# Matmul, GELU, matmul on one core: another order for the first contraction slices of the first product

## The chip, the core and the metric

The kernel runs on one core of a Trainium2 chip. The core has five engines with queues of their own: TensorE (PE, with weight loads as PEld), VectorE (DVE), ScalarE (ACT), GpSimd (POOL) and SyncE (SP). They meet through semaphores. DMA transfers are issued from SP's and POOL's queues here. The metric is the device time of one execution in microseconds (us); a kernel's figure is the median over its runs.

## The reference

```python
m, k, n, p = 1024, 1024, 2048, 1024        # a: m x k, b: k x n, c: n x p, all fp32
h = np.matmul(a, b)
h = 0.5 * h * (1 + np.tanh(np.sqrt(2 / np.pi) * (h + 0.044715 * h ** 3)))
return np.matmul(h, c).astype(np.float32)
```

## The kernel before

Everything is computed transposed: `hT`, the hidden matrix with its 2048 columns on the partitions, in 16 tiles of 128, and the 1024 rows of `a` as two halves of 512 (index `h`, 0 and 1). The contraction of the first product has 8 slices of 128 (`k`). `aT[:, h, k]` is a slice of a half, transposed; `b1[:, k]` holds the first 1024 columns of `b`, `b2` the others, `c_sb` all of `c`, in bf16.

There are three stages, in an order written out by hand: each engine runs its instructions in the order in which the program names them.

1. Hidden tiles 0 to 7 (from `b1`) for both halves, by ordinary matmuls (`mm1`, line 126): 8 tiles x 8 slices x 2 halves = 128 matmuls of 128x128 by 128x512. GELU on ACT writes `hT`.
2. Hidden tiles 8 to 15 (from `b2`) by a scheme with seven products in place of eight (class `Seven`, function `seven`; the matmuls are at line 229). Its sums and differences `t1` to `t4` (of parts of `aT`) and `s1` to `s4` (of parts of `b2`) are DVE work. `t1`, `t2` and `t3` are done in stage 1.
3. The second product, by the same scheme.

Stage 1 is what the change concerns. Its input comes in two ways. SP's queue loads fp32 data into staging tiles (`sta` for `a`, `stb` for `b`), and DVE or ACT cast it to bf16 (lines 118, 135, 136). POOL's queue loads with a cast to bf16 on the way, straight into `b1`, `b2`, `c_sb` and the pieces `a1` (lines 98, 105, 109, 112). The copy at line 85, into `gate`, makes POOL wait for SP's load of slice 1 of `b` before it issues the first of its own.

A slice of `a` is transposed on PE, four transposes of 128x128 for 512 rows, into a PSUM bank (`pt`), and DVE copies the bank into `aT` (`turn0`, line 116, for staged slices; `turn`, line 154, for two slices loaded by POOL). PSUM has eight banks, and a tile takes a whole one; a bank is used again when its reader is done.

The order before: slices 0 to 3 of half 0 for tiles 0 to 6, slice by slice as they arrive through SP, into seven banks; these sums leave PSUM for `half` (`leave`, line 145), tile 7 following. Then half 1: all eight slices, from POOL's loads, with GELU from PSUM. Then half 0's slices 4 to 7, each tile's sum added to `half` on DVE (line 258) and passed through GELU. SP loads slices 0 to 3 of half 0 of `a` and slices 0 to 3 of `b1`; POOL all else.

After stage 1, `seven` begins with four products into banks `X` (snapped to SBUF by ACT, line 268), then four into banks `Y`, to which DVE adds the snapped ones (line 273).

Of the kernel before, what the change touches and what calls it, by code (L numbers as in the profile page):

```python
# [9 lines left out]
F32 = mybir.dt.float32  # L10
F32R = mybir.dt.float32r
BF16 = mybir.dt.bfloat16
AF = mybir.ActivationFunctionType
ADD = mybir.AluOpType.add
# [5 lines left out]
def kernel(ctx, tc, a, b, c, out):  # L20
    nc = tc.nc
# [3 lines left out]
    H = 512  # L25
    KT = K // 128
    NT = N // 128

    av = a.rearrange("(mt p) k -> p mt k", p=128)
    bv = b.rearrange("(kt p) n -> p kt n", p=128)  # L30
# [9 lines left out]
    def slot(tag, shape, dt, name):  # L40
        return big.tile(shape, dt, name=name, tag=tag)

    def bank(i, shape=(128, H), dt=F32, name="ps"):
        return pp.tile(list(shape), dt, name=name, tag=f"bank{i}", padded_shape=None)

    def pieces(tag, bufs, shape, dt, name):
        return small.tile(shape, dt, name=name, tag=tag, bufs=bufs)
# [3 lines left out]
    ident = consts.tile([128, 128], BF16, name="ident")  # L51
    make_identity(nc, ident)
    gate = consts.tile([128, 1], F32, name="gate")
# [4 lines left out]
    aT = slot("a", [128, 2, KT, H], BF16, "aT")  # L58
    b1 = slot("b1", [128, KT, 1024], BF16, "b1")
    b2 = slot("b2", [128, KT, 1024], BF16, "b2")  # L60


    N0 = 7
    stb = slot("x0", [128, 4, 1024], F32, "stb")
    sta = slot("x1", [128, 4096], F32, "sta")

    def slice_a(k, n):
        return sta[:, ds(k * H, n * H)].rearrange("p (mt c) -> p mt c", mt=4)

    def load_a(k, n):  # L70
        nc.sync.dma_start(out=slice_a(k, n), in_=av[:, 0:4, ds(k * 128, n * 128)])  # L71

    def load_b(k, c0=0, w=1024):
        nc.sync.dma_start(out=stb[:, k, ds(c0, w)], in_=bv[:, k, ds(c0, w)])  # L74

    load_a(0, 1)
    load_b(0, 0, H)
    load_b(0, H, H)
    load_a(1, 1)
    load_b(1)  # L80
    load_a(2, 2)
    load_b(2)
    load_b(3)

    nc.gpsimd.tensor_copy(gate, stb[:, 1, 0:1])  # L85
    nc.scalar.activation(g, warm[:, 0:1], AF.Gelu_apprx_tanh)
    wps = bank(7, name="warmps")
    for _ in range(8):
        nc.tensor.matmul(wps, warm[:, 0:128], warm, start=True, stop=True)


    KH = KT // 2

    def load_half(h, k0):
        sts = []
        for j in range(0, 4, 2):
            st = pieces("m", 4, [128, 2, H], BF16, "a1")
            nc.gpsimd.dma_start(out=st, in_=av[:, 4 * h + j:4 * h + j + 2, ds(k0 * 128, H)])  # L98
            sts.append(st)
        return sts  # L100

    a10 = load_half(1, 0)
    a11 = load_half(1, KH)
    for k in range(KH, KT):
        nc.gpsimd.dma_start(out=b1[:, k], in_=bv[:, k, 0:1024])
    a01 = load_half(0, KH)
    for n in range(2):
        for k in range(0, KT, 4):
            nc.gpsimd.dma_start(out=b2[:, k:k + 4, ts(n, H)],
                                in_=bv[:, k:k + 4, ds(1024 + n * H, H)])  # L110
    for t in range(0, NT, 2):
        nc.gpsimd.dma_start(out=c_sb[:, t:t + 2], in_=cv[:, t:t + 2])  # L112

    ps = [bank(t) for t in range(N0)]

    def turn0(k, n):
        ab = pieces("ab", 2, [128, 4, n * 128], BF16, "ab")
        nc.vector.tensor_copy(ab, slice_a(k, n))
        pt = bank(7, (128, n, H), BF16, "pt")
        for i in range(n):  # L120
            for j in range(4):
                nc.tensor.transpose(pt[:, i, ts(j, 128)], ab[:, j, ts(i, 128)], ident)
        for i in range(n):
            nc.vector.tensor_copy(aT[:, 0, k + i], pt[:, i])

    def mm1(p, t, h, ks, k0=0, k1=KT):
        for k in ks:
            nc.tensor.matmul(p, b1[:, k, ts(t, 128)], aT[:, h, k],  # L128
                             start=(k == k0), stop=(k == k1 - 1))

    turn0(0, 1)
    for k in range(KH):
        for c0 in (0, 256) if k == 0 else (0,):
            w = 256 if k == 0 else H
            nc.scalar.activation(b1[:, k, ds(c0, w)], stb[:, k, ds(c0, w)], AF.Copy)  # L135
        nc.vector.tensor_copy(b1[:, k, H:], stb[:, k, H:])
        for t in range(N0):
            mm1(ps[t], t, 0, (k,), 0, KH)
        if k < 2:
            turn0(k + 1, k + 1)  # L140


    half = slot("x3", [128, 8, H], F32, "half")

    def leave(t, p):
        if t in (1, 3, 5):
            nc.vector.tensor_copy(half[:, t], p)
        else:
            nc.scalar.activation(half[:, t], p, AF.Copy)

    for t in range(N0):
        leave(t, ps[t])

    def turn(sts, h, k, i):
        pt = bank(i, (128, 2, H), BF16, "pt")
        for n in range(2):
            for j in range(4):
                nc.tensor.transpose(pt[:, n, ts(j, 128)],  # L158
                                    sts[j // 2][:, j % 2, ts((k + n) % KH, 128)], ident)
        nc.vector.tensor_copy(aT[:, h, k:k + 2], pt)  # L160

    def gelu(t, h, p):
        nc.scalar.activation(hT[h][:, t], p, AF.Gelu_apprx_tanh)  # L163

    turn(a10, 1, 0, 0)
    p7 = bank(7)
    mm1(p7, 7, 0, range(KH), 0, KH)
    leave(7, p7)
    turn(a10, 1, 2, 1)
    B1 = (2, 3, 4, 5, 6, 7, 0, 1)  # L170
    ps = []
    for t in range(3):
        ps.append(bank(B1[t]))
        mm1(ps[t], t, 1, range(2))
    for t in range(3):
        mm1(ps[t], t, 1, range(2, KH))


    class Seven:
# [47 lines left out]
        def product(self, p, l, r, j, start, c0=0, w=H):  # L227
            for k in range(self.kt):
# [4 lines left out]
    x = [slot(f"x{i}", [128, 2, 4, H], F32R, "x1") for i in range(3)]  # L233
    one = Seven(4, [[b2[:, 0:4, 0:H], b2[:, 4:8, 0:H]], [b2[:, 0:4, H:], b2[:, 4:8, H:]]],
                [[aT[:, 0, 0:4], aT[:, 1, 0:4]], [aT[:, 0, 4:8], aT[:, 1, 4:8]]],
                [x[i][:, 0] for i in range(3)] + [None], [x[i][:, 1] for i in range(3)] + [None])
    one.t1()

    for t in range(3, 8):
        if t == 5:  # L240
            turn(a11, 1, KH, 0)
            turn(a11, 1, KH + 2, 1)
        ps.append(bank(B1[t]))
        mm1(ps[t], t, 1, range(KH))
    one.t3()
    one.t2()


    for t in range(8):
        mm1(ps[t], t, 1, range(KH, KT))  # L250
        gelu(t, 1, ps[t])
        if t in (3, 5):
            turn(a01, 0, KH + t - 3, B1[t - 3])
    C1 = (3, 5, 2, 4, 6, 7, 0, 1)
    for t in range(8):
        p = bank(C1[t])
        mm1(p, t, 0, range(KH, KT), KH)
        nc.vector.tensor_tensor(out=half[:, t], in0=p, in1=half[:, t], op=ADD)  # L258
        gelu(t, 0, half[:, t])
    x.append(slot("x3", [128, 2, 4, H], F32R, "x1"))  # L260
    one.s[3], one.t[3] = x[3][:, 0], x[3][:, 1]

    X = (2, 3, 4, 5)
    Y = (6, 7, 0, 1)

    def snap(tag, p, name):
        st = pieces(tag, 4, [128, H], F32, name)
# [8 lines left out]
    def seven(w, done, between):  # L276

        (A11, A12), (A21, A22) = w.A
        (B11, B12), (B21, B22) = w.B
        px = [bank(i) for i in X]  # L280
        p1, v, u = {}, {}, {}
# [4 lines left out]
        for j in range(4):  # L286
            p = bank(Y[j])
            w.product(p, A12, B21, j, True)
            done(0, 0, j, plus(p, p1[j]))
        between("P2")  # L290
        py = [bank(i) for i in Y]
        for j in range(4):
# [119 lines left out]
```

## Time and profile before

| | us |
|---|---|
| median of 6 runs | 122.08 (121.64 to 123.05) |
| the profiled execution | 121.93 |
| its span | 120.2 |
| PE busy | 111.3 (93%) |
| DVE busy | 89.1 (74%) |
| ACT busy | 50.8 (42%) |
| POOL busy | 16.3 (14%) |

The span is the time between the first and the last instruction that the profile shows; the execution's own time is 1.7 us longer. Busy shares are means over stages with different limits: PE is seldom idle after the first part, so that DVE's 74% says nothing on its own. What a change in stage 1 is worth is read from the waits in stage 1 and from what follows it without a gap. By the page, PE's clock is granted in full in all 40 slices of the span. 16.34 MB moved by DMA, of which POOL's queue took 8.91 MB and SP's 7.34 MB, the stores among the latter.

In an answer of the timeline a line has the start in us, the duration in us, the engine, the line of the kernel, the operation with output and inputs, and in brackets the engine's idle time before it with what ended that. A pipelined group of matmuls is one line, with its count.

### The profile page before, as it was taken

Reading aid. Unit: us, or ns where it says so; the run is one execution under the profiler, and the core shown is the slowest. Engines: PE = TensorE matmul, PEld = TensorE weight load, DVE = VectorE, ACT = ScalarE, POOL = GpSimd, SP = SyncE. Lnnn points to the kernel's source line nnn. Section 1 sums busy time; section 2 is a strip of 40 time slices with the busy share of each in tenths; the row PEclk is TensorE's granted clock in tenths of the full one; section 3 lists DMA queues with packets and bytes.
Section 4 is the critical chain, followed back from the end, with each engine's and each line's share of the span. In section 5 each row is a group of like instructions: output and inputs, shape, how many; then the busy total and the mean of one; then the engine's idle time right before and its main releaser. Section 6 shows DMA issues by size and latency. Waiting matters only on the chain.

```text
span 120.2 us, 1435 instructions
## 1 busy us (share of the span) xinstructions
PE 111.3 (93%) x536; PEld 71.3 (59%) x536; DVE 89.1 (74%) x97; ACT 50.8 (42%) x82; POOL 16.3 (14%) x29
## 2 busy tenths in 40 slices
PE   6775889999999999999999999999999999999970
PEld 2122445644544445888887444468888888888840
DVE  0235587497338899977779999969999996892480
ACT  4112461006547689946769536900012595100000
POOL 2008907843243000000000000000000000000000
PEclk9999999999999999999999999999999999999999
DMA  3799999999999999998000000072000002004695
GB/s 97 196 343 393 161 168 210 208 203 206 206 207 212 210 214 209 211 212 159 4 3 0 0 5 0 0 262 87 0 0 0 0 5 87 0 0 175 242 350 193
DMA packets 11110, 16.34 MB, mean 136 GB/s; under 512 B 736, under 2 KB 5856, under 8 KB 11104
## 3 DMA queue, kind: packets, MB, share of 16 engines
q0 software_dynamic: 6496, 8.91, 42.5%
q1 hardware_dynamic: 4608, 7.34, 17.2%
q8 instruction: 4, 0.07, 0.2%
q14 instruction: 2, 0.02, 0.0%
HBM read 20.97 MB, written 4.19 MB: 209 GB/s over the span
## 4 chain that ended last, share of the span: by engine, by line
PE 71%; DMA 16%; DVE 6%; SPq 1%; issue 1%; POOL 1%; ACT 1%; DVEq 0%; ACTq 0%
PE ps L229 51%; PE ps L128 18%; DMA stb<-in_b_dram 6%; DMA out_dram<-ot 5%; DMA a<-in_a_dram 5%; DVE x L187 4%; PE pt L158 2%; DVE ot L273 2%; SPq L74 1%; SPq L71 1%; POOL a L98 1%; DVE ot L358 1%; ACT u L268 1%; POOL gate L85 0%; DVEq L273 0%
## 5 line engine op out<-in xcount | busy, mean ns | idle before, releaser
L128 PE MATMUL ps<-aT,b 128*128 128x512 bf16 x128 | 29.1, 379 | 3.1 <-ACT b L135 2.1
L229 PE MATMUL ps<-x,s 128*128 128x512 f32 x128 | 29.6, 391 | 0.0
L229 PEld LDWEIGHTS ps<-x,s 128*128 128x128 f32 x128 | 24.0, 188 | 5.1
L128 PEld LDWEIGHTS <-b 128*128 128x128 bf16 x128 | 12.1, 98 | 17.0 <-ACT b L135 3.2
L229 PE MATMUL ps<-x,x 128*128 128x512 f32 x64 | 14.8, 389 | 0.0
L229 PE MATMUL ps<-c_sb,hT 128*128 128x512 bf16 x64 | 14.0, 379 | 0.0
L229 PEld LDWEIGHTS ps<-x,x 128*128 128x128 f32 x64 | 12.0, 188 | 2.5
L268 ACT ACTIVATE v<-ps 128x512 f32<-128x512 f32 x8 | 4.8, 599 | 17.1 <-PE ps L229 17.1
L163 ACT ACTIVATE hT<-ps 128x512 bf16<-128x512 f32 x12 | 6.8, 594 | 11.3 <-PE ps L128 11.3
L229 PE MATMUL ps<-x 128*128 128x512 f32 x48 | 11.3, 394 | 0.0
L229 PEld LDWEIGHTS <-hT 128*128 128x128 bf16 x64 | 6.2, 98 | 7.6 <-issue 0.3
L229 PEld LDWEIGHTS ps<-x 128*128 128x128 f32 x48 | 9.0, 188 | 2.0
L187 DVE TENSOR_TENSOR x<-c_sb 128x1024 fp32r<-128x1024 bf16 x8 | 9.2, 1216 | 0.0
L273 DVE TENSOR_TENSOR ot<-ps,v 128x512 f32<-128x512 f32 x8 | 5.3, 686 | 4.6 <-DMA out_dram<-ot 3.8
L258 DVE TENSOR_TENSOR half<-ps,half 128x512 f32<-128x512 f32 x8 | 5.5, 692 | 3.2 <-PE ps L128 2.9
L160 DVE COPY aT<-pt 128x1024 bf16<-128x1024 bf16 x6 | 4.1, 689 | 5.1 <-PE pt L158 5.1
L273 DVE TENSOR_TENSOR ot<-ps,u 128x512 f32<-128x512 f32 x8 | 5.4, 691 | 3.0 <-ACT u L268 3.0
L163 ACT ACTIVATE hT<-ot 128x512 bf16<-128x512 f32 x12 | 6.9, 623 | 1.1 <-DVE ot L273 1.1
L229 PE MATMUL ps<-aT,b 128*128 128x512 bf16 x32 | 7.1, 379 | 0.0
L112 POOL DMA_DIRECT2D c_sb<-in_c_dram x8 | 5.7, 713 | 9.8 <-DMA b<-in_b_dram 8.9
L268 ACT ACTIVATE p<-ps 128x512 f32<-128x512 f32 x8 | 4.6, 594 | 4.8 <-PE ps L229 4.8
L135 ACT ACTIVATE b<-stb 128x512 bf16<-128x512 f32 (+1 forms) x5 | 2.6, 541 | 9.2 <-DMA stb<-in_b_dram 9.2
(45 smaller groups left out, 114.6 us busy)
## 6 DMA issues: line engine op xcount, KB each, us to landing
c_sb<-in_c_dram POOLq DMA_DIRECT2D x8, 512.0 KB, 19.6
out_dram<-ot SPq DMA_DIRECT2D x16, 256.0 KB, 2.1
b<-in_b_dram POOLq DMA_DIRECT2D x4, 512.0 KB, 12.6
stb<-in_b_dram SPq DMA_DIRECT2D x3, 512.0 KB, 8.5
a<-in_a_dram POOLq DMA_DIRECT2D x6, 256.0 KB, 7.2
b<-in_b_dram POOLq DMA_DIRECT2D x4, 256.0 KB, 9.1
sta<-in_a_dram SPq DMA_DIRECT2D x2, 256.0 KB, 4.2
stb<-in_b_dram SPq DMA_DIRECT2D x2, 256.0 KB, 4.9
```

What stands on the lines that cost most here:

```text
L71: nc.sync.dma_start(out=slice_a(k, n), in_=av[:, 0:4, ds(k * 128, n * 128)])
L112: nc.gpsimd.dma_start(out=c_sb[:, t:t + 2], in_=cv[:, t:t + 2])
L128: nc.tensor.matmul(p, b1[:, k, ts(t, 128)], aT[:, h, k], start=(k == k0), stop=(k == k1 - 1))
L135: nc.scalar.activation(b1[:, k, ds(c0, w)], stb[:, k, ds(c0, w)], AF.Copy)
L158: nc.tensor.transpose(pt[:, n, ts(j, 128)], sts[j // 2][:, j % 2, ts((k + n) % KH, 128)], ident)
L160: nc.vector.tensor_copy(aT[:, h, k:k + 2], pt)
L163: nc.scalar.activation(hT[h][:, t], p, AF.Gelu_apprx_tanh)
L187: nc.vector.tensor_tensor(out=dst[:, r], in0=x[:, r], in1=y[:, r], op=op)
L229: nc.tensor.matmul(p[:, ds(c0, w)], l[:, k, ts(j, 128)], r[:, k, ds(c0, w)], start=(start and k == 0), stop=(k == self.kt - 1), skip_group ...
L258: nc.vector.tensor_tensor(out=half[:, t], in0=p, in1=half[:, t], op=ADD)
L268: nc.scalar.activation(st, p, AF.Copy)
L273: nc.vector.tensor_tensor(out=ot, in0=p, in1=st, op=ADD)
```

## The change

Stage 1 takes its work in another order, with other loads. Stage 2 and 3 differ only in the banks `X` and `Y`.

- Half 0 goes first with one slice only, slice 0, for all eight tiles (`first`); these sums go to `half`.
- Then half 1 with all eight slices, tiles 0 to 6 slice by slice (`begin`, and the loop from 2 to `KT`), tile 7 at the end.
- Then slices 1 to 7 of half 0 (`rest`), added to `half` as before.
- SP now loads slice 0 of half 0 of `a`, all slices of half 1 and all eight slices of `b1`, in fp32; DVE and ACT cast them. A second staging tile for `b` takes the place of `x2`. The last piece of `a` for half 1 reuses the place of the first two in `sta`.
- POOL loads slices 1 to 7 of half 0 of `a`, then `b2` and `c` as before. The copy into `gate` waits for slice 5 of `b`.
- `t3` stands behind the loop, `t1` and `t2` behind the last transposes of half 0.

```diff
-    stb = slot("x0", [128, 4, 1024], F32, "stb")
+    stb = [slot(f"x{i}", [128, 4, 1024], F32, "stb") for i in (0, 2)]
+    at = {(0, 0): 0, (1, 0): 1, (1, 1): 2, (1, 2): 3, (1, 4): 5, (1, 6): 0}
...
-    load_a(0, 1)
+    load_a(0, 0, 1)
     load_b(0, 0, H)
+    load_a(1, 0, 1)
     load_b(0, H, H)
-    load_a(1, 1)
+    load_a(1, 1, 1)
     load_b(1)
-    load_a(2, 2)
+    load_a(1, 2, 2)
     load_b(2)
     load_b(3)
-
-    nc.gpsimd.tensor_copy(gate, stb[:, 1, 0:1])
+    load_a(1, 4, 2)
+    load_b(4)
+    load_b(5)
+
+    nc.gpsimd.tensor_copy(gate, stb[1][:, 1, 0:1])
...
+    a0 = {}
+    for k, n in ((1, 3), (4, 4)):
         for j in range(0, 4, 2):
+            st = pieces("v", 4, [128, 2, n * 128], BF16, "a0")
+            nc.gpsimd.dma_start(out=st, in_=av[:, j:j + 2, ds(k * 128, n * 128)])
...
+    def turn(h, k, n, i, get):
+        pt = bank(i, (128, n, H), BF16, "pt")
+        for m in range(n):
+            for j in range(4):
+                nc.tensor.transpose(pt[:, m, ts(j, 128)], get(k + m, j), ident)
+        nc.vector.tensor_copy(aT[:, h, k:k + n], pt)
+
+    def cast_a(h, k, n):
         ab = pieces("ab", 2, [128, 4, n * 128], BF16, "ab")
+        nc.vector.tensor_copy(ab, slice_a(h, k, n))
+        return lambda q, j: ab[:, j, ts(q - k, 128)]
+
+    def turn_cast(h, k, n, i):
+        turn(h, k, n, i, cast_a(h, k, n))
...
+    def first(t, i):
+        p0[t] = bank(i)
+        mm1(p0[t], t, 0, (0,), 0, 1)
+
+    def begin(t, i, ks):
+        p1[t] = bank(i)
+        mm1(p1[t], t, 1, ks)
+
+    turn_cast(0, 0, 1, 7)
+    cast_b(0, 0, 256)
+    cast_b(0, 256, 256)
+    for t in range(4):
+        first(t, t)
+        leave(t, p0[t])
+    turn_cast(1, 0, 1, 6)
+    for t, i in enumerate((4, 5, 7, 6)):
+        begin(t, i, (0,))
+    cast_b(0, H, H, nc.vector)
+    a11 = cast_a(1, 1, 1)
+    for t in range(4, 8):
+        first(t, t - 4)
+    leave(4, p0[4])
+    leave(5, p0[5], nc.vector)
+    begin(4, 0, (0,))
+    cast_b(1, 0, H)
+    turn(1, 1, 1, 1, a11)
+    cast_b(1, H, H, nc.vector)
+    leave(6, p0[6])
+    leave(7, p0[7], nc.vector)
+    for t in range(5):
+        mm1(p1[t], t, 1, (1,))
+    begin(5, 1, (0, 1))
+    begin(6, 2, (0, 1))
+    turn_cast(1, 2, 2, 3)
+    load_a(1, 6, 2)
+    load_b(6)
+    load_b(7)
+    for k in range(2, KT):
+        cast_b(k, 0, H)
+        cast_b(k, H, H, nc.vector)
+        for t in range(7):
+            mm1(p1[t], t, 1, (k,))
+            if k == KT - 1:
+                gelu(t, 1, p1[t])
+        if k in (3, 5):
+            turn_cast(1, k + 1, 2, 3)
...
+    one.t3()
+    begin(7, 4, range(KT))
+    gelu(7, 1, p1[7])
...
+    turn(0, 1, 1, 3, get)
+    turn(0, 2, 2, 5, get)
+    R = (7, 6, 0, 1, 5, 4, 3, 2)
+    for t in range(4):
+        rest(t, R[t], (1,))
+    for t in range(4):
+        rest(t, R[t], (2, 3))
+    turn(0, 4, 2, 3, get)
+    turn(0, 6, 2, 2, get)
     one.t1()
-    for t in range(3, 8):
-        if t == 5:
-            turn(a11, 1, KH, 0)
-            turn(a11, 1, KH + 2, 1)
...
     one.t2()
+    rest(4, R[4], (1, 2, 3))
     for t in range(8):
+        rest(t, R[t], range(1 if t > 4 else 4, KT))
+        nc.vector.tensor_tensor(out=half[:, t], in0=p0r[t], in1=half[:, t], op=ADD)
         gelu(t, 0, half[:, t])
...
-    X = (2, 3, 4, 5)
-    Y = (6, 7, 0, 1)
+    X = (7, 6, 0, 1)
+    Y = (5, 4, 3, 2)
```

More of the change, by code (lines that the diff above doesn't have):

```diff
@@ L60, with slice_a, load_a @@
     b2 = slot("b2", [128, KT, 1024], BF16, "b2")
-    N0 = 7
-    stb = slot("x0", [128, 4, 1024], F32, "stb")
+    stb = [slot(f"x{i}", [128, 4, 1024], F32, "stb") for i in (0, 2)]
     sta = slot("x1", [128, 4096], F32, "sta")
[L67 to L71, printed above, removed]
+    at = {(0, 0): 0, (1, 0): 1, (1, 1): 2, (1, 2): 3, (1, 4): 5, (1, 6): 0}
+    def slice_a(h, k, n):
+        return sta[:, ds(at[h, k] * H, n * H)].rearrange("p (mt c) -> p mt c", mt=4)
+    def load_a(h, k, n):
+        nc.sync.dma_start(out=slice_a(h, k, n), in_=av[:, 4 * h:4 * h + 4, ds(k * 128, n * 128)])
     def load_b(k, c0=0, w=1024):
-        nc.sync.dma_start(out=stb[:, k, ds(c0, w)], in_=bv[:, k, ds(c0, w)])
-    load_a(0, 1)
+        nc.sync.dma_start(out=stb[k // 4][:, k % 4, ds(c0, w)], in_=bv[:, k, ds(c0, w)])
+    load_a(0, 0, 1)
     load_b(0, 0, H)
+    load_a(1, 0, 1)
     load_b(0, H, H)
-    load_a(1, 1)
+    load_a(1, 1, 1)
     load_b(1)
-    load_a(2, 2)
+    load_a(1, 2, 2)
     load_b(2)
     load_b(3)
-    nc.gpsimd.tensor_copy(gate, stb[:, 1, 0:1])
+    load_a(1, 4, 2)
+    load_b(4)
+    load_b(5)
+    nc.gpsimd.tensor_copy(gate, stb[1][:, 1, 0:1])
     nc.scalar.activation(g, warm[:, 0:1], AF.Gelu_apprx_tanh)
@@ L89 @@
         nc.tensor.matmul(wps, warm[:, 0:128], warm, start=True, stop=True)
-    KH = KT // 2
-    def load_half(h, k0):
-        sts = []
+    a0 = {}
+    for k, n in ((1, 3), (4, 4)):
         for j in range(0, 4, 2):
[L97 to L106, printed above, removed]
+            st = pieces("v", 4, [128, 2, n * 128], BF16, "a0")
+            nc.gpsimd.dma_start(out=st, in_=av[:, j:j + 2, ds(k * 128, n * 128)])
+            for i in range(2):
+                for m in range(n):
+                    a0[k + m, j + i] = st[:, i, ts(m, 128)]
     for n in range(2):
@@ L112, with cast_b @@
         nc.gpsimd.dma_start(out=c_sb[:, t:t + 2], in_=cv[:, t:t + 2])
-    ps = [bank(t) for t in range(N0)]
-    def turn0(k, n):
-        ab = pieces("ab", 2, [128, 4, n * 128], BF16, "ab")
[L118 to L124, printed above, removed]
+    def turn(h, k, n, i, get):
+        pt = bank(i, (128, n, H), BF16, "pt")
+        for m in range(n):
+            for j in range(4):
+                nc.tensor.transpose(pt[:, m, ts(j, 128)], get(k + m, j), ident)
+        nc.vector.tensor_copy(aT[:, h, k:k + n], pt)
+    def cast_a(h, k, n):
+        ab = pieces("ab", 2, [128, 4, n * 128], BF16, "ab")
+        nc.vector.tensor_copy(ab, slice_a(h, k, n))
+        return lambda q, j: ab[:, j, ts(q - k, 128)]
+    def turn_cast(h, k, n, i):
+        turn(h, k, n, i, cast_a(h, k, n))
+    def cast_b(k, c0, w, eng=None):
+        src, dst = stb[k // 4][:, k % 4, ds(c0, w)], b1[:, k, ds(c0, w)]
+        if eng is nc.vector:
+            nc.vector.tensor_copy(dst, src)
+        else:
+            nc.scalar.activation(dst, src, AF.Copy)
     def mm1(p, t, h, ks, k0=0, k1=KT):
@@ L129, in mm1, with leave @@
                              start=(k == k0), stop=(k == k1 - 1))
[L131 to L140, printed above, removed]
     half = slot("x3", [128, 8, H], F32, "half")
-    def leave(t, p):
-        if t in (1, 3, 5):
+    def leave(t, p, eng=None):
+        if eng is nc.vector:
             nc.vector.tensor_copy(half[:, t], p)
@@ L149, in leave @@
             nc.scalar.activation(half[:, t], p, AF.Copy)
[L151 to L160, printed above, removed]
     def gelu(t, h, p):
         nc.scalar.activation(hT[h][:, t], p, AF.Gelu_apprx_tanh)
[L165 to L176, printed above, removed]
+    p0, p1 = {}, {}
+    def first(t, i):
[42 more added lines that the diff above has]
+            turn_cast(1, k + 1, 2, 3)
     class Seven:
@@ L236, with get, rest @@
                 [x[i][:, 0] for i in range(3)] + [None], [x[i][:, 1] for i in range(3)] + [None])
-    one.t1()
-    for t in range(3, 8):
-        if t == 5:
-            turn(a11, 1, KH, 0)
-            turn(a11, 1, KH + 2, 1)
-        ps.append(bank(B1[t]))
-        mm1(ps[t], t, 1, range(KH))
-    one.t3()
+    one.t3()
+    begin(7, 4, range(KT))
+    gelu(7, 1, p1[7])
+    def get(k, j):
+        return a0[k, j]
+    def rest(t, i, ks):
+        if t not in p0r:
+            p0r[t] = bank(i)
+        mm1(p0r[t], t, 0, ks, 1)
+    p0r = {}
+    turn(0, 1, 1, 3, get)
[7 more added lines that the diff above has]
+    turn(0, 6, 2, 2, get)
+    one.t1()
     one.t2()
+    rest(4, R[4], (1, 2, 3))
     for t in range(8):
[L250 to L258, printed above, removed]
+        rest(t, R[t], range(1 if t > 4 else 4, KT))
+        nc.vector.tensor_tensor(out=half[:, t], in0=p0r[t], in1=half[:, t], op=ADD)
         gelu(t, 0, half[:, t])
```

## The prediction

> **What bounds the kernel now.** I read the chain of waits first, to see which stretch is paced by what. Columns: start us, us, what.
>
> ```profile
> 2.72 6.71 DMA stb<-in_b_dram
> ...
> 10.69 6.12 DMA a<-in_a_dram
> ...
> 23.89 6.04 PE ps L128 x28
> ...
> 32.55 8.63 PE ps L128 x40
> 41.18 60.71 PE ps L229 x272
> ```
>
> Until 16.8 us loads set the pace; then TensorE works without a gap to 101.9. The 272 products of the second stage go at 60.71 / 272 = 0.223 us each: a later first product (line 229) makes the end later by as much, unless it fills a gap, and there is none. So one number decides: when that first product starts. The PE's timeline (start us, us, engine, line, operation) says when, and what happened before:
>
> ```profile
> 4.94 0.40 PE L122 MATMUL pt<-ident,ab 128*128 128x128 bf16 x4
> 6.18 1.04 PE L128 MATMUL ps<-aT,b 128*128 128x512 bf16 x4 [0.84 <-ACT b L135]
> 7.67 0.82 PE L128 MATMUL ps<-aT,b 128*128 128x512 bf16 x3 [0.45 <-DVE b L136]
> 8.46 0.40 PE L122 MATMUL pt<-ident,ab 128*128 128x128 bf16 x4
> 10.14 1.69 PE L128 MATMUL ps<-aT,b 128*128 128x512 bf16 x7 [1.29 <-ACT b L135]
> 11.99 0.62 PE L122 MATMUL pt<-ident,ab 128*128 128x128 bf16 x8 [0.16 <-DVE ab L118]
> 13.12 3.18 PE L128 MATMUL ps<-aT,b 128*128 128x512 bf16 x14 [0.52 <-DVE aT L124]
> ...
> 41.02 7.07 PE L229 MATMUL ps<-aT,b 128*128 128x512 bf16 x32
> ```
>
> The first product starts at 41.02. Fourteen matmuls take 3.18 with the last one's own 0.38, so one costs (3.18 - 0.38) / 13 = 0.2155; a transpose costs (0.62 - 0.22) / 7 = 0.057. From 8.46 to 41.02, 121 matmuls (26.1) and 60 transposes (3.4) are done, so stalls are 32.56 - 29.5 = 3.1 us: 2.4 of it the waits in brackets and that for `a` at 16.86 (0.44), the rest drained pipelines. There is little to win.
>
> The DVE timeline gives the prices that matter:
>
> ```profile
> 7.97 0.43 DVE L118 CAST ab<-sta 128x512 bf16<-128x512 f32 x1 [0.36 <-DMA sta<-in_a_dram]
> 8.89 0.42 DVE L124 COPY aT<-pt 128x512 bf16<-128x512 bf16 x1 [0.49 <-PE pt L122]
> 11.02 0.91 DVE L118 CAST ab<-sta 128x1024 bf16<-128x1024 f32 x1 [1.14 <-DMA sta<-in_a_dram]
> ...
> 17.41 0.69 DVE L160 COPY aT<-pt 128x1024 bf16<-128x1024 bf16 x1 [0.26 <-PE pt L158]
> ```
>
> Windows of half a microsecond give the DMA rate (last two columns: DMA share, GB/s):
>
> ```profile
> 3.50:4.00 0.50, 0.50 (x3) 0.15 (x1) 0.43 (x1) 0.00 (x0) 0.00 (x0) 1.00 0.63 53
> 7.50:8.00 0.50, 0.33 (x2) 0.21 (x3) 0.14 (x2) 0.00 (x0) 0.00 (x0) 1.00 0.98 299
> 10.00:10.50 0.50, 0.36 (x2) 0.21 (x3) 0.00 (x0) 0.09 (x1) 0.50 (x1) 1.00 1.05 422
> 12.00:12.50 0.50, 0.50 (x8) 0.43 (x8) 0.00 (x0) 0.26 (x1) 0.50 (x2) 1.00 0.82 143
> ```
>
> Summing such windows and comparing with the waits for SP's loads: the bytes of `b` slice 1 are in at 8.06 and its user starts at 9.46; the next `a` piece 9.45 and 11.02; slice 2 10.72 and 12.24. So a load lands some 1.4 us after its bytes.
>
> **What the Trainium skill says.** "TensorE: Matmul & The Clock Gate", Part 2, Step-by-step: only weight loads are pulled ahead, matmuls stay in program order. So a matmul waiting for a transposed slice holds everything behind it. The trace agrees: at 12.92 weights are loaded while the matmuls wait for the copy until 13.12. "DMA: Bandwidth & Descriptors", Issuing engines are not separate DMA queues: SP's and POOL's transfers share the same engines. The trace agrees: the rate drops from 422 to 143 GB/s when SP's loads give way to POOL's (which read fp32 and are counted as bf16 written). The same page, Anatomy of one DMA: a fixed cost of about 2 us, mostly completion; here I see the 1.4 above.
>
> **The change part by part.** Matmuls and transposes are the same in number (128 and 64). What moves is the order. I walk it with the prices above, 0.03 from PE to DVE (transposes end 8.86, copy 8.89) and about 0.05 back (cast ends 8.40, transposes 8.46).
>
> Loads. SP's list grows from 3.15 to 6.55 MB: all of `b1` and the whole second half of `a`, plus one slice of the first half. Cumulated after the old rates (0.42 MB/us for `b`, about 0.32 for 512-byte pieces of `a`) plus 1.4: `a` (1,0) about 7.15, `b` 0's second half 7.9, `a` (1,1) 8.7, `b` 1 10.1, `a` (1,2) 11.4, `b` 2 12.7, `b` 3 13.9, `a` (1,4) 15.3, `b` 4 16.5, `b` 5 17.8, `a` (1,6) 19.2, `b` 6 20.4, `b` 7 21.7, up to 23.3 if POOL's traffic takes half. The (1,6) piece waits at SP, with `b` 6 and 7 behind it, for casts done by 7.6, ahead of its turn: nothing. POOL's gate moves to `b` 5: its loads start at 18.3 instead of 9.9, and four for the rest of `a` go first (0.72 each); bytes at 0.4 MB/us, they land at about 24 and 26.5. `b2` follows by about 37, `c` at the old time, since the bytes read are the same.
>
> Start. The first slice is as before: four matmuls at 6.18. Then `a` (1,0): cast 7.18 to 7.61, transposes 7.65, copy 8.09 to 8.51, four matmuls of the second half at 8.56. Before stood at 8.46 with three more matmuls done and four fewer transposes: 0.1 + 0.65 - 0.23 = 0.52 lost. ACT's four evacuations (2.06 for four) hide behind this.
>
> First stalls. `first(4..7)` ends 10.29. `begin(4)` reuses bank 0, so it waits for `leave(4)` (mm end 9.83 + 0.60): 0.19. The turn of (1,1) waits for `leave(5)` on DVE (10.05 to 10.68): 0.03; then copy 11.16 to 11.58, and five matmuls at 11.62: stall 0.66. Two `begin` of two matmuls fill 12.70 to 13.56.
>
> The three turns of two slices, (1,2), (1,4), (1,6): each stands directly ahead of matmuls that need it. Transposes issue in 0.45, the last result comes 0.2 later, copy 0.69, semaphores: the stall is 0.93 each, 2.8 together. Casts for them are covered: (1,2) is cast 12.63 to 13.54, after `leave(7)` and just in time. So matmuls run 14.96 to 17.98, 19.36 to 22.38, 23.76 to 26.78. Every load above is there before its cast would hold a matmul, by 0.8 us (`b` 1) or more and by 1.3 for a late `b` 7, so the extra casts (ACT 0.63, DVE 0.43 a slice) cost nothing; without that cover, its lateness one for one.
>
> Rest. `begin(7)` to 28.5, turn of (0,1): stall 0.21, as the second turn covers most. `rest` for four tiles to 31.98; the last turns are covered by three matmuls of tile 4. The two late loads are 4.5 and 5.5 us early. `t1` and `t2` on DVE end at 38.4 and the eight additions, at about 0.62 back to back as at line 273 (four in 2.48), end at 43.4, with the last matmul at 42.4 anyway; DVE's `s1`, `s2` and first sum follow to 48.6, and the product that needs that bank comes at 49.3. So no stall there, by 0.7 (before: 0.6).
>
> Sum of stalls after 8.56: 0.19 + 0.03 + 0.66 + 0.02 + 2.8 + 0.21 = 3.9, against 3.1. First product: 8.56 + 124 x 0.2155 + 56 x 0.057 + 3.9 = 42.4; semaphores and a slightly later first `a` piece make it 42.5. That is 1.5 later: 121.93 of the profiled execution (span 120.2 and 1.7 around it) + 1.5 = 123.4. The median of the runs is 122.08, 0.15 above the profiled one; on it, 123.6. I take 123.4.
>
> **Unknown costs.** `a` (1,0) goes third, with four times as many pieces as the `b` load that stood there. The near row is the 3.5 to 4.0 window: 53 GB/s. At best it lands where the old third load did (7.13), at worst a second such gap costs 1 us. I take 7.2. The additions: 0.62 to 0.69, the second eats the margin of 0.7 and costs nothing more. POOL against SP: between no delay and 1.6 us, under the margin.
>
> **Rivals.** (1) The stalls as above: 122.8 to 124.2, chance 0.67. (2) Loads come late: a second gap in the early stream shifts the whole chain from `a` (1,0) on, since nothing in the order absorbs it. For: the 53 GB/s window, small pieces. Against: from 5 us on the stream never fell below 280. 1 us more: 124.4, chance 0.17. (3) Not slower: TensorE doesn't stand still in the three pair turns, because DVE's copy is shorter or overlaps the transposes. Place: the matmuls behind (1,2), (1,4), (1,6). It decides from where the three cost 0.48 each instead of 0.93: then 3.9 falls to 2.55, the first product comes at 41.1 and the time is 122.0; hidden wholly, at 39.7 and 120.6. For: at 13.12 before, matmuls waited 0.52 after a turn. Against: there the copy was in two parts of one slice, here it is one of 0.69. Chance 0.16, a third of it below the bound.
>
> **How the numbers follow.** About 0.5% (0.61 us) is what a measurement can tell. Faster, below 121.47: 0.05, from (3). Same, to 122.69: 0.11, from (3). Slower: 0.84, from (1) and (2). The likeliest is (1), 123.4. The range takes in the stall and stream bounds: 122.3 to 124.8, leaving most of (3) and the bad end of (2) out.
>
> **What would show it.** PE should have three waits on the copy into `aT` of about 0.7 (0.93 with the drained pipe), one of 0.5 after (1,1), the first product near 42.5 and 60.7 us of products behind it. ACT's and DVE's casts of `b` should release no matmul after 12 us. Wrong would be: waits of PE on casts or loads after 12, a first product before 41.6, or a gap among the products.

## The result, and the profile after

The changed kernel takes 124.41 us (median of 28 executions) where the kernel before takes 122.50 (63); the ratio is 1.0113, with a 95% interval of 1.0087 to 1.0139. On the 121.93 us that the forecast started from, that is 123.3 us. The two medians lie further apart (by 1.9 us, 1.6%), because this ratio, like those below, leaves out executions more than 1.5% above the fastest of their kernel, 11 of the 28 here and 14 of the 63 by the same cut. Executions of both kernels scatter by several us. Each kernel has two profiles here; the difference between its two arises in the first 15 us, and some 79.2 us pass from the first product to the end of the span in all four. So single times say little here, and stretches of the profile behind the start say much.

The profiled execution has a span of 122.7, against 120.2. Its chain of waits (start us, us, what), the lines that answer to those of before:

```profile
1.21 4.81 DMA stb<-in_b_dram
...
12.30 0.44 DVE aT L116
...
15.37 0.70 DVE aT L116
...
19.78 0.70 DVE aT L116
...
24.18 0.70 DVE aT L116
...
34.23 9.51 PE ps L135 x44
43.74 60.70 PE ps L249 x272
```

The second wait for a load (`a`, 6.12 us from 10.69) is gone from the chain; in its place stand DVE's copies into `aT`. The 272 products take 60.70, as before (60.71), so all of the difference is made ahead of the first one. The PE's timeline shows where:

```profile
1.19 3.59 PE L93 MATMUL warmps<-warm 128*128 128x512 bf16 x8 [1.19 <-DVE warm L50]
4.93 0.58 PE L115 MATMUL pt<-ident,ab 128*128 128x128 bf16 x4
6.51 1.89 PE L135 MATMUL ps<-aT,b 128*128 128x512 bf16 x4 [1.00 <-ACT b L131]
8.19 0.63 PE L115 MATMUL pt<-ident,ab 128*128 128x128 bf16 x4
9.34 2.60 PE L135 MATMUL ps<-aT,b 128*128 128x512 bf16 x9 [0.52 <-DVE aT L116]
11.88 0.38 PE L115 MATMUL pt<-ident,ab 128*128 128x128 bf16 x4
12.78 2.10 PE L135 MATMUL ps<-aT,b 128*128 128x512 bf16 x9 [0.52 <-DVE aT L116]
14.72 0.61 PE L115 MATMUL pt<-ident,ab 128*128 128x128 bf16 x8
16.11 3.18 PE L135 MATMUL ps<-aT,b 128*128 128x512 bf16 x14 [0.78 <-DVE aT L116]
19.13 0.61 PE L115 MATMUL pt<-ident,ab 128*128 128x128 bf16 x8
20.52 3.18 PE L135 MATMUL ps<-aT,b 128*128 128x512 bf16 x14 [0.78 <-DVE aT L116]
23.54 0.61 PE L115 MATMUL pt<-ident,ab 128*128 128x128 bf16 x8
24.93 4.91 PE L135 MATMUL ps<-aT,b 128*128 128x512 bf16 x22 [0.78 <-DVE aT L116]
...
43.58 7.07 PE L249 MATMUL ps<-aT,b 128*128 128x512 bf16 x32
```

Three times the eight transposes of two slices are followed by a wait of 0.78 for the copy; with the 0.15 in which the last transpose drains, 0.93 is lost each time. The first four matmuls behind the transposes take 1.89 where the kernel before needed 1.04: here TensorE keeps the half pace of its eight warming matmuls (line 93) until about 10 us, while the kernel before had the full pace at 4.94. The first product starts at 43.58 instead of 41.02. All that TensorE waited for (us in total, times, longest):

```profile
PE ps L135 <- DVE aT L116: 3.4, 5, 0.8
PE warmps L93 <- DVE warm L50: 1.2, 1, 1.2
PE ps L135 <- ACT b L131: 1.0, 1, 1.0
```

The one wait for a cast is the first matmul's, at 6.51. After that no load and no cast holds TensorE.

### The profile page after: what moved, and what is told of

Its sections match the earlier page's. It is cut to its first block, busy times and chain, and to the rows that moved or that the text cites. A ratio compares the mean times of both kernels' runs of the same rounds, so it can differ in the third digit from the quotient of the medians.

```text
span 122.7 us, 1443 instructions
## 1 busy us (share of the span) xinstructions
PE 113.1 (92%) x536; PEld 72.2 (59%) x536; DVE 90.3 (74%) x103; ACT 52.8 (43%) x87; POOL 12.6 (10%) x23
## 4 chain that ended last, share of the span: by engine, by line
PE 77%; DVE 10%; DMA 7%; issue 1%; ACT 1%; SPq 0%; DVEq 0%; ACTq 0%
PE ps L249 49%; PE ps L135 25%; DMA stb<-in_b_dram 4%; DVE x L207 4%; DMA out_dram<-ot 3%; DVE aT L116 3%; PE pt L115 3%; DVE ot L386 2%; DVE ot L301 2%; ACT u L296 0%; ACT b L131 0%; SPq L71 0%; DVEq L301 0%; DVEq L386 0%; ACTq L296 0%
## 5 line engine op out<-in xcount | busy, mean ns | idle before, releaser
L135 PE MATMUL ps<-aT,b 128*128 128x512 bf16 x128 | 30.3, 389 | 4.5 <-DVE aT L116 3.4
L116 DVE COPY aT<-pt 128x1024 bf16<-128x1024 bf16 (+1 forms) x10 | 5.8, 583 | 14.3 <-PE pt L115 14.3
L131 ACT ACTIVATE b<-stb 128x512 bf16<-128x512 f32 (+1 forms) x9 | 5.1, 580 | 10.3 <-DMA stb<-in_b_dram 10.3
L147 ACT ACTIVATE hT<-half 128x512 bf16<-128x512 f32 x8 | 4.8, 630 | 9.4 <-DVE half L286 9.4
L147 ACT ACTIVATE hT<-ps 128x512 bf16<-128x512 f32 x12 | 6.1, 612 | 4.1 <-PE ps L135 4.1
L249 PE MATMUL ps<-aT,b 128*128 128x512 bf16 x32 | 7.1, 379 | 0.0
```

What stands on the lines that cost most here:

```text
L116: nc.vector.tensor_copy(aT[:, h, k:k + n], pt)
L131: nc.scalar.activation(dst, src, AF.Copy)
L135: nc.tensor.matmul(p, b1[:, k, ts(t, 128)], aT[:, h, k], start=(k == k0), stop=(k == k1 - 1))
L249: nc.tensor.matmul(p[:, ds(c0, w)], l[:, k, ts(j, 128)], r[:, k, ds(c0, w)], start=(start and k == 0), stop=(k == self.kt - 1), skip_group ...
```

## The experiments

A measure almost free of the start is the stretch from the transposes of slice (1,1) to the first product: 11.88 to 43.58, 31.70 us, in the changed kernel. The forecast's sum gives 10.73 to 42.37, 31.64.

### Turns one slice earlier

```diff
     begin(5, 1, (0, 1))
-    begin(6, 2, (0, 1))
     turn_cast(1, 2, 2, 3)
+    begin(6, 2, (0, 1))
...
-        cast_b(k, 0, H)
-        cast_b(k, H, H, nc.vector)
+        if k % 2 == 0:
+            for q in (k, k + 1):
+                cast_b(q, 0, H)
+                cast_b(q, H, H, nc.vector)
...
-        if k in (3, 5):
-            turn_cast(1, k + 1, 2, 3)
+        if k in (2, 4):
+            turn_cast(1, k + 2, 2, 3)
```

> The changed kernel with the three turns of two slices one slice earlier, so that DVE's copy into aT runs beside other matmuls; loads, casts and counts are the same. Theory (the copies stand exposed on TensorE's path, 0.93 us each): the waits on the copies of (1,4) and (1,6) vanish, that of (1,2) falls from 0.93 to about 0.5; first product 2.3 us earlier than in the changed kernel, time 1.9% below it, ratio to the kernel before about 0.993. Rival (the loads pace this stretch anyway): the waits return as waits on casts or loads, gain under 0.7 us, ratio above 1.005.

Its PE timeline:

```profile
6.68 1.04 PE L135 MATMUL ps<-aT,b 128*128 128x512 bf16 x4 [1.21 <-ACT b L131]
...
8.53 3.79 PE L135 MATMUL ps<-aT,b 128*128 128x512 bf16 x9 [0.52 <-DVE aT L116]
...
15.99 1.67 PE L135 MATMUL ps<-aT,b 128*128 128x512 bf16 x7 [0.35 <-DVE aT L116]
17.50 0.61 PE L115 MATMUL pt<-ident,ab 128*128 128x128 bf16 x8
17.95 3.18 PE L135 MATMUL ps<-aT,b 128*128 128x512 bf16 x14
20.97 0.61 PE L115 MATMUL pt<-ident,ab 128*128 128x128 bf16 x8
21.42 6.42 PE L135 MATMUL ps<-aT,b 128*128 128x512 bf16 x29
...
41.59 4.70 PE L251 MATMUL ps<-aT,b 128*128 128x512 bf16 x21
```

Behind the last two turns no wait is left, and 0.35 behind the first. The stretch from (1,1), which starts at 12.15 here, is 29.44: 2.26 shorter than in the changed kernel, where 2.3 was forecast. So the three copies do stand on the path, at the price given. The time falls less: 122.68 us, ratio 1.006 (1.0033 to 1.0088), 0.005 (some 0.65 us) below the changed kernel's, where 0.993 was expected. That part of the expectation failed. The experiment with both edits shows what stands in the way: with a start 0.7 us earlier than here, the first product comes at 41.48, and here at 41.59, so in these two profiles a quicker start gains almost nothing once the turns are moved.

### Copies split by slice

```diff
-        nc.vector.tensor_copy(aT[:, h, k:k + n], pt)
+        for m in range(n):
+            nc.vector.tensor_copy(aT[:, h, k + m], pt[:, m])
```

> The changed kernel with each two-slice copy into aT split in two of one slice (0.42 us each in place of one of 0.69). Theory: the matmuls of the first slice of a pair wait for 0.42 instead of 0.69, the second copy hides behind seven matmuls: 0.27 us less in each of three turns, 0.8 us in all, ratio to the kernel before about 1.005. Rival (something else than the copy's length holds the matmuls): no gain, ratio 1.011.

The PE timeline of this kernel, behind the three turns:

```profile
14.50 3.18 PE L136 MATMUL ps<-aT,b 128*128 128x512 bf16 x14 [0.52 <-DVE aT L117]
...
18.64 3.18 PE L136 MATMUL ps<-aT,b 128*128 128x512 bf16 x14 [0.51 <-DVE aT L117]
...
22.79 4.91 PE L136 MATMUL ps<-aT,b 128*128 128x512 bf16 x22 [0.52 <-DVE aT L117]
```

Each wait is 0.26 shorter (0.78 to 0.52), about the 0.27 by which the copy is shorter (0.69 to 0.42). The stretch (10.37 to 41.43) is 31.06, 0.64 less; a wait for the cast of `b` 1, 0.68 in place of one of 0.52, took 0.16 of the 0.8. This execution is at (1,1) 1.5 us earlier than the changed kernel's, with the same loads, and still TensorE waits for none behind slice 1. Ratio 1.0066 (1.0028 to 1.0103), expected 1.005.

### A load more

```diff
     load_b(3)
+    nc.sync.dma_start(out=stb[1][:, 3], in_=bv[:, 0, 1024:2048])
     load_a(1, 4, 2)
```

> The changed kernel with a load of 512 KB that nothing reads, in SP's queue between slice 3 of b and slice 4 of a: all later loads land about 1.25 us later. Theory (loads have 1.3 us or more to spare from there on): no change against the changed kernel, ratio to the kernel before 1.009 to 1.014, still no wait of TensorE on a cast or load after 12 us. Rival (the stream of loads paces it): about 1.2 us more, ratio about 1.021.

The stretch (12.65 to 44.36) is 31.71: 512 KB more in the stream change nothing. TensorE's waits for the copies are the same:

```profile
PE ps L136 <- DVE aT L117: 3.4, 5, 0.8
```

Ratio 1.0123 (1.0051 to 1.0195). This execution started 0.8 us later than the changed kernel's profile, which gave the later loads as much more time; the added load should cost them about 1.25. With the quick start of the experiment before, in which they held nothing either, that is enough to say that the loads behind slice 3 aren't on the path, and the rival falls for this part of the stream. Ahead of it the landing of `a` (1,0) does move: in the profiles with that order its cast starts between 6.73 and 8.05.

### Gaps filled with matmuls

```diff
+    fill = bank(5, name="fill")
+    def busy(n):
+        for _ in range(n):
+            nc.tensor.matmul(fill, warm[:, 0:128], warm, start=True, stop=True)
     turn_cast(0, 0, 1, 7)
+    busy(2)
...
+    busy(2)
     turn_cast(1, 0, 1, 6)
+    busy(2)
```

> The changed kernel with six matmuls that nothing reads, put into TensorE's first gaps: two ahead of the first products, two ahead of the turn of (1,0) and two behind it. In the profile of the changed kernel the first matmuls took about twice as long as in that of the kernel before (four in 1.89 us in place of 1.04), which is 1.1 us of its 2.5. Theory A (this is chance of the run, not the order): the six cost between nothing and 0.5 us, ratio 1.011 to 1.015, slow and quick starts in about the old shares. Theory B (the gaps in the new order keep TensorE's early rate low): with the gaps filled the quick start returns in every execution, ratio about 1.005, and the slower half of the executions (above 124.3 us) vanishes.

Ratio 1.0124 (1.008 to 1.0169), so against theory B's 1.005 the average gains nothing that shows. But its six executions lie between 123.30 and 124.36, none with a mean granted clock under 0.99, where those of the changed kernel go up to 126.07. Windows from 9 to 12 us (the clock is the third figure from the end) of this kernel, and of the kernel with earlier turns:

```profile
9.00:12.00 3.00, 2.88 (x15) 1.25 (x14) 1.80 (x4) 1.28 (x3) 0.00 (x0) 1.00 1.07 397
```

```profile
9.00:12.00 3.00, 3.00 (x8) 1.06 (x7) 0.84 (x2) 1.45 (x4) 0.00 (x0) 0.50 1.06 396
```

At half clock TensorE does 8 matmuls there, where the filled kernel does 15 (transposes and fillers among them). That is what the kernel with earlier turns lost in its profile: nine matmuls in 3.79 us instead of 2.30. The pace isn't all of the start, though. In the filled kernel's profile it was full, but the load of `a` (1,0) came late, and the first matmul of half 1 started at 9.45, no earlier than in the changed kernel (9.34):

```profile
8.05 0.43 DVE L120 CAST ab<-sta 128x512 bf16<-128x512 f32 x1 [2.54 <-DMA sta<-in_a_dram]
...
9.45 2.30 PE L135 MATMUL ps<-aT,b 128*128 128x512 bf16 x9
```

The stretch from (1,1) is 31.71 with filled gaps too.

### Earlier turns and filled gaps

The two edits together.

> The kernel with turns one slice earlier, and the six filling matmuls as well. In the profiles of that kernel and of the one with the extra load, the granted clock falls to 0.5 from about 9 to 12 us, after a gap of TensorE; in the filled kernel it doesn't. Theory: with the gaps filled the clock holds (no execution below 0.99), the slow start of 1.2 to 1.5 us goes, first product at 40.5 to 41.2 and ratio 0.995 to 1.0, spread of the executions about 1 us. Rival (with a quick start the loads of a (1,4) to b 7 come late): waits on casts or loads between 15 and 25 us, ratio 1.003 to 1.006.

122.34 us, ratio 1.0013 (0.9984 to 1.0043): the time of the kernel before. 14 executions lie between 121.91 and 123.06, none under 0.99 in clock. Its interval still meets that of the earlier turns alone (1.006), and 0.995 to 1.0 was expected. The stretch (11.44 to 41.48) is 30.04, not 29.44: with the early start the loads begin to count. Two of them show, each worth 0.3: the cast of `a` (1,6), on which the last pair turn waits, and the first transposes of half 0:

```profile
19.80 0.69 DVE L120 CAST ab<-sta 128x1024 bf16<-128x1024 f32 x1 [1.00 <-DMA sta<-in_a_dram]
...
27.67 0.56 PEld L115 LDWEIGHTS <-a 128*128 128x128 bf16 x10 [0.31 <-DMA a<-in_a_dram]
```

POOL's load of slices 1 to 3 lands at 27.6 here, just as it is wanted. Both theories hold half: no execution lost the clock, and the loads are the next limit.

### Two loads swapped

```diff
     load_a(0, 0, 1)
-    load_b(0, 0, H)
     load_a(1, 0, 1)
+    load_b(0, 0, H)
...
     turn_cast(0, 0, 1, 7)
+    turn_cast(1, 0, 1, 6)
...
-    turn_cast(1, 0, 1, 6)
```

> The changed kernel with the second load and third load of SP's queue swapped (slice 0 of a for half 1 ahead of the first half of slice 0 of b), and its turn ahead of the first products. Theory (the chain of cast, transposes, copy behind a (1,0) is what the start waits for, so its landing shifts all): the first matmuls of half 1 start at 8.0 to 8.5 instead of 8.1 to 9.5, and the time falls by 0.3 to 0.8 us against the changed kernel, ratio 1.005 to 1.010. Rival (the bytes of the first three loads set the start in any order): no change, ratio 1.011 to 1.014.

124.41 us, ratio 1.0145 (1.0081 to 1.0209): no gain shows, where 1.005 to 1.010 was expected. The cast of `a` (1,0) starts at 5.90, but what it overtook comes later, and so does the next piece, as its DVE timeline shows:

```profile
8.55 0.43 DVE L129 CAST b<-stb 128x512 bf16<-128x512 f32 x1 [1.11 <-DMA stb<-in_b_dram]
...
10.40 0.43 DVE L120 CAST ab<-sta 128x512 bf16<-128x512 f32 x1 [1.42 <-DMA sta<-in_a_dram]
```

Slice (1,1) is cast at 10.40 instead of 9.54. The rival, that the bytes and not their order set the start, fits better, but this doesn't decide it: the interval reaches into both ranges, and TensorE took 4.41 us for the first 13 matmuls, where the full pace gives about 3.0 (12 x 0.2155 + 0.38). The stretch behind it is 31.70.

### All three, and the changed kernel again

> All three edits together: turns one slice earlier, filling matmuls, swapped loads. Theory: the gains add up as far as the loads allow: first product at 40.0 to 41.0, ratio 0.99 to 0.998, faster than both kernels. Rival (loads pace it once the stalls are gone): waits on casts or loads between 15 and 25 us, same as without the swap.

This version has four filling matmuls, not six. 122.85 us, ratio 1.005 (1.0025 to 1.0075): the swap gains nothing (1.0013 without it, the intervals overlap), and 0.99 to 0.998 was expected. As the rival had it, the transposes wait for casts of `a`, 1.1 us in three.

> The changed kernel unchanged, beside the others: ratio 1.009 to 1.014 again, executions spread over 3 us, some of them with a mean granted clock below 0.99 (one stretch of 3.4 us at half rate is 0.014 of the span), and a stretch from the turn of (1,1) to the first product of 31.7 us whatever the start.

Ratio 1.0104 (1.0027 to 1.0181), executions from 122.96 to 126.02, stretch 31.70 (13.38 to 45.08). This profile has the late start at its worst: first matmuls at 6.97, nine matmuls in 3.75.

### The kernel before, filled, and seen again

```diff
     turn0(0, 1)
+    busy(7, 2)
...
             turn0(k + 1, k + 1)
+        if k == 0:
+            busy(7, 3)
```

> The kernel before with five filling matmuls that nothing reads: two behind the first turn, three behind the second. It asks whether the early rate is lost by gaps in the kernel before too. Theory (a gap of TensorE above about 1 us in the first 12 us can halve the rate for 3.4 us, in any kernel): the slow executions above 123 us go, none has a mean clock below 0.99, median 0.3 to 0.7 us under the kernel before, ratio of the quick ones 0.997 to 1.002. Rival (only the changed order suffers): median and spread as those of the kernel before.

122.34 us, ratio 1.0005 (0.9981 to 1.003), against 122.44 for the kernel before beside it. The clock was under 0.99 in 1 of 22 executions, against 12 of 43 without the fillers; yet one took 126.0, and a gain in time, for which 0.3 to 0.7 us was expected, isn't shown.

> The kernel before unchanged, one more look at its start: the second turn's transposes between 8.2 and 9.0 us, and from there to the first product 32.6 us if the early matmuls run at full rate, up to 1.5 more if they don't.

The second turn starts at 9.14, a little later than expected, and 33.60 us later the first product, with seven matmuls in 3.17 us in place of 1.69. These matmuls, and two windows:

```profile
10.93 3.17 PE L128 MATMUL ps<-aT,b 128*128 128x512 bf16 x7 [1.15 <-ACT b L135]
...
9.00:12.00 3.00, 1.85 (x8) 0.90 (x8) 1.06 (x3) 0.63 (x1) 1.73 (x3) 0.50 1.00 394
12.00:15.00 3.00, 2.95 (x13) 1.50 (x12) 0.73 (x2) 1.26 (x2) 3.00 (x6) 0.51 0.91 169
```

So the half clock meets the kernel before as well; the profile that the forecast used had none of it.

### Split copies on top, and loads in the order of use

> The changed kernel with turns one slice earlier, filling matmuls and copies split by slice. Theory: of the stalls of the changed kernel, the one ahead of slice 2 (0.57 left) falls by 0.27, those ahead of 4 and 6 are hidden already: 0.2 to 0.3 us below the kernel without the split, ratio 0.996 to 1.001. Rival (late loads pace it by now): no change, ratio 1.000 to 1.003.

Ratio 1.0028 (1.0006 to 1.0051): no gain over the kernel without the split, as the rival had it. What TensorE waited for:

```profile
PE pt L115 <- DVE ab L121: 1.2, 2, 0.7
```

The turns of (1,4) and (1,6) now wait for casts whose loads have just landed. So the loads are what is left, and their order was tried. Two more things change with it: the staging tile is one piece longer, so that the last piece of `a` need not wait for a place in it, and DVE casts two pieces of `a` ahead of a slice of `b`:

```diff
-    sta = slot("x1", [128, 4096], F32, "sta")
-    at = {(0, 0): 0, (1, 0): 1, (1, 1): 2, (1, 2): 3, (1, 4): 5, (1, 6): 0}
+    sta = slot("x1", [128, 4608], F32, "sta")
+    at = {(0, 0): 0, (1, 0): 1, (1, 1): 2, (1, 2): 3, (1, 4): 5, (1, 6): 7}
...
     load_b(2)
-    load_b(3)
     load_a(1, 4, 2)
+    load_b(3)
     load_b(4)
+    load_a(1, 6, 2)
     load_b(5)
...
-    load_a(1, 6, 2)
     load_b(6)
...
                 cast_b(q, H, H, nc.vector)
+                if q in (2, 4):
+                    ab = cast_a(1, q + 2, 2)
...
-            turn_cast(1, k + 2, 2, 3)
+            turn(1, k + 2, 2, 3, ab)
```

> The kernel with earlier turns, filling matmuls and split copies, and besides in SP's queue slices 4 and 5 of a (half 1) ahead of slice 3 of b, slices 6 and 7 of a ahead of slice 5 of b (a staging tile one piece longer, so that they wait for nothing), and DVE's casts of them ahead of those of slices 3 and 5 of b. In the profile without this, the transposes waited 0.58 and 0.65 us for these casts, whose loads had just landed. Theory (with the stalls gone the order of the loads paces it): these two waits go, one of 0.3 to 0.6 on a cast of b comes in their place, first product 0.6 to 0.9 us earlier, at about 40.8, ratio 0.995 to 0.999. Rival (the bytes, not their order): waits of the same sum elsewhere, ratio 1.001 to 1.004.

What TensorE waited for, and the first product:

```profile
PE ps L137 <- ACT b L133: 1.4, 3, 0.6
...
41.21 5.13 PE L263 MATMUL ps<-aT,b 128*128 128x512 bf16 x23
```

The waits for `ab` are gone; of the 1.4 for casts of `b`, 0.83 are new (0.40 and 0.43), the rest is the first matmul's. 121.66 us against 122.57 for the kernel before beside it, ratio 0.9944 (0.9917 to 0.997): the one version here that is faster than both. The profile carries only part of this. Its first product, at 41.21, is 0.38 earlier than without the new order (41.59), where 0.6 to 0.9 was expected, and the execution took 122.20 us, one of the longer of the 22. What the quicker ones gain besides wasn't seen, nor which of the three parts of the edit does it.

## Why the prediction was right

Of the signs that it named, the waits came as told: three of 0.78 on the copies, 0.52 behind (1,1), none on a cast or load after 12 us, no gap among the products. The first product didn't: 43.58, not near 42.5.

- **The end follows the first product.** Right: 60.70 us for 272 products, and the span grew by 2.5, the first product came 2.56 later.
- **Three pair turns at 0.93.** Right and shown: 0.78 of wait and 0.15 of drain each, three times; moving them saved 2.26 of the 2.8, as forecast for that move; shortening the copy by 0.27 shortened each wait by 0.26.
- **0.66 behind (1,1), 0.21 behind (0,1), no stall later.** Right within 0.1: from (1,1) to the first product 31.70, forecast 31.64. DVE's eight additions went back to back, and the sum that frees the bank ran from 48.91 to 49.6, 0.7 ahead of the products that take it at 50.30, as forecast:

```profile
39.56 4.92 DVE L286 TENSOR_TENSOR half<-ps,half 128x512 f32<-128x512 f32 x8
44.39 2.28 DVE L207 TENSOR_TENSOR x<-b 128x2048 fp32r<-128x2048 bf16 x1
46.71 2.29 DVE L207 TENSOR_TENSOR x<-x,b 128x2048 fp32r<-128x2048 f32 x1
48.91 2.54 DVE L301 TENSOR_TENSOR ot<-ps,p 128x512 f32<-128x512 f32 x4
```

- **Loads and casts are covered.** Right for this order: no wait for them after the first matmul, and 512 KB more cost nothing. The cast of the last slice of `b` began at 22.16, between the forecast's 21.7 and the 23.3 with half the rate lost to POOL. (The drop from 422 to 143 GB/s, which the prediction puts beside the shared engines, shows only that POOL's loads are counted at a lower rate; it doesn't show the sharing.) POOL's first load went at 18.30, as forecast, but what its loads of `a` take from issue to landing varies: 4.7 to 7.8 us here, and 4.3 to 8.8 with earlier turns and filled gaps, where the last of slices 1 to 3 came at 27.6, and not at the forecast's 24. The changed kernel wants them at 29.7 and never waited. Once the stalls are taken out the cover is gone, as the four versions with earlier turns and filled gaps show. The two-slice cast is 0.69, not 0.91; it was covered either way.
- **The start.** Here the sum is off in the profile: half 1's first matmul at 9.34, not 8.56, and the transposes of (1,1) 2.54 later, not 2.17. Together that is 1.15, all of the 1.1 by which the first product missed 42.5. The landing of `a` (1,0) wasn't the cause in this execution (its cast began at 6.86, before the 7.18 assumed); the first cast of `b` came 0.33 later than before, and the matmuls and transposes up to 10 us ran at half pace. The forecast took the early pace of one profile of the kernel before for granted, and the kernel before loses it too at times. So it is in part luck that the ratio falls within 0.1 us of the forecast: the plain medians differ by 1.9 us, not 1.5, and the 2.6 of the two profiles hold 1.15 that the forecast knew nothing of. Whether the new order makes a late start more frequent, and why TensorE came to its full pace late here, stays open.
- **The rivals.** The stream of loads wasn't what made the changed kernel slower. The one on the other side, with hidden copies, wasn't this kernel, but it could be made: hiding and splitting them, filling the gaps and putting loads and casts in the order of their use gave 0.9944.

## What to carry to other kernels

A transposition directly ahead of the matmuls that need it costs the drain, the copy and two handovers, here 0.93 us for two slices, whatever the engines' busy shares; one other slice of matmuls in between hides it. Compare the stretch behind the disturbed start, not only the whole times: it came out as 31.70 or 31.71 in five profiles with these turns and unsplit copies, where the times scatter by 3 us. When a stall is taken away, look at the order of the loads next: here the first gain stopped at the kernel before's time, and new orders of loads and casts brought the rest.

## What the runs showed of the hardware

- TensorE's clock can fall back to half for 3 us and more after it had been full, with gaps of only about a microsecond: in the kernel with earlier turns four matmuls took 1.04 us at 6.68, behind a gap of 1.21, and the window from 9 to 12 shows 0.50. In the second profile of the kernel before the windows from 9 to 15 show 0.50 and 0.51. Six matmuls without a reader in the gaps kept the mean at 0.99 or more in all 64 executions of four versions; in a fifth, with the swapped loads and four of them, one of 22 fell. That the gaps cause it is what these runs suggest; the threshold wasn't measured.
- The recorded clock doesn't account for every slow matmul: in the changed kernel's profile it reads 1.00 throughout, while four matmuls took 1.89 us in place of 1.04. The eight warming matmuls take 3.3 to 3.6 us in every profile, where the full pace gives about 1.9 (7 x 0.2155 + 0.38), and the record reads 1.00 there too.
- The first loads land irregularly: the cast of `a` (1,0), which waits for its load, began between 6.73 and 8.05 in kernels with the same order up to there.
